# The weights' remainders formed by accumulating DMAs instead of VectorE subtractions, in a two-layer fp32 transformer trunk

## The chip, the cores and the metric

One NeuronCore of a Trainium2 chip. The metric is the device time of one execution in microseconds; for the kernel before it is the median of three runs. The kernel's engines are TensorE (PE: matmuls, and transposes), VectorE (DVE), ScalarE (ACT), GpSimd (POOL) and SyncE (SP), which issues most DMAs.

## The reference

Two layers of a trunk over 512 tokens of 1024 features, in fp32. Each layer has a mixing part and an FFN:

```python
xn = rmsnorm(x, norm1_g[i])
u_pool, q, k, v, g_a, g_b = split(xn @ w_in[i])
# q, k: rmsnorm over 128 features, rotary on the first 32; 4 heads, two softmaxes per head
attn = concat(rmsnorm(softmax1 @ v - lam * softmax2 @ v, subln_g[i])) * (1 - lam_init)   # masked by chunks of 64
pool = (window means of u_pool - u_pool, windows 2, 4, 8, 16) @ pool_w[i] * pool_scale[i]
x = x + (sigmoid(g_a) * pool + sigmoid(g_b) * attn) @ w_out[i]
gate, up = split(rmsnorm(x, norm2_g[i]) @ w_ffn_in[i])                                    # 2 x 2816
x = x + (silu(gate) * up) @ w_ffn_out[i]
```

## The kernel before

**Three matmuls for one product.** The kernel does every fp32 product as three matmuls of a rounded format (fp32r), in which a value keeps 12 significant bits. A value is split into a rounded part, hi, and the remainder lo = value - hi; `product` (L207) adds the stationary operand's hi by the moving one's hi (L215), its hi by the moving one's lo (L216), and its lo by the moving one's hi (L217); the weights are the stationary operand in some products and the moving one in others, as in `w_out`. In a matmul's row the moving operand comes first. So each weight is needed as `whi` and `wlo`.

**The weights.** The host lays all weights out in the order of their use, as 244 pieces of two row tiles by 512 columns, 512 KB each (`weight_plan`). `piece` (L175) loads the next one: a DMA on SP into a tile `raw` (L180, three buffers; the first four pieces lie elsewhere), then `split` (L164): ACT copies `raw` to `whi`, which rounds it (L166), and DVE subtracts, `wlo = raw - whi` (L167). `whi` and `wlo` have eight buffers each, so a piece is split once TensorE is done with the piece eight places earlier. `wblock` gives a block: eight row tiles (four pieces) of `w_in` or `w_ffn_in`; for `w_out` one piece by column half for a single head, and two for the last two heads; the FFN's down projection takes four or three pieces by column half. `split` is also used for activations, so the lines L166 and L167 hold both; the tile's name tells them apart (`whi`/`wlo` are weights).

**The order of the work.** In each layer the heads go in the order 3, 2, 1, 0: `attention` makes q, k, v and the gate of one head, and the steps of its softmax chain are put off by `later` until TensorE has streamed so many columns (`QK_WAIT` and the like), so that TensorE has other matmuls meanwhile. `mix` of the head before makes the pool branch (u; its gate as `ta` by a Tanh on ACT, L485), its product with `pool_w`, then on DVE `ta` by the product (L493) and the sum of both branches (L494), split into `mh` on ACT (L172) and `ml` on DVE (L173), the stationary operands of `w_out` (`project_out`, `add_out`). `project_out` comes for head 3, for head 2 each alone, and for the last two together, after `mix(3)`. Then the FFN in three rounds (`ffn_in`, `swiglu`, `ffn_out`). The program gives this order; a scheduler then sets each engine's own order from it, and an engine takes its instructions strictly in that order.

**The norms** use POOL: DVE makes the mean square (r, L230), POOL raises it to the power -0.5 (L231, "pow"), and DVE scales by it (for q and k: L422, after ACT's squares in L418, then rotary in L286 to L291, and TensorE's transposes, L221). Apart from constants at the start these 80 pows are all that POOL does before the change.

Of the kernel before, what the change touches and what calls it, by code (L numbers as in the profile page):

```python
# [12 lines left out]
AF = mybir.ActivationFunctionType  # L13
ALU = mybir.AluOpType
# [12 lines left out]
ROT = 32  # L27
# [3 lines left out]
EPS = 1e-6  # L31
WINDOWS = (2, 4, 8, 16)
MASKED = -3.0e38
# Hidden tiles of the FFN in three rounds.
ROUNDS = ((0, 8), (8, 16), (16, 22))
# Rows of `rows`, per layer: q gain, k gain, lambda vectors, sub-norm gain.
R_QG, R_LAM, R_SG = 0, 256, 768
ORDER = (3, 2, 1, 0)
# The hidden tiles lie where the attention's tiles lay: from which tile on, under which tag, how many.
HIDDEN_AT = {0: ("qk", 4), 4: ("v", 2), 6: ("u", 2), 8: ("m", 2), 10: ("qk", 4), 14: ("v", 2), 16: ("u", 2), 18: ("m", 2),  # L40
             20: ("qk", 4)}
# How many columns TensorE streams between a step and the one of its chain that follows on TensorE.
QK_WAIT, SCORE_WAIT, PROB_WAIT, AV_WAIT, NORM_WAIT, MERGE_WAIT = 20400, 33600, 25200, 11400, 15000, 15000


def weight_plan():
    """The weight pieces in the order of their use: (name, layer, first row tile, columns)."""
    plan = []

    def block(name, layer, cols, k0=0, k1=KD):  # L50
        for k in range(k0, k1, 2):
            plan.append((name, layer, k, cols))

    def span(*parts):
        return [c for a, n in parts for c in range(a, a + n)]

    def qk(j):
        return span((1024 + 256 * j, 256), (2048 + 256 * j, 256))

    def vg(j):  # L60
        return span((3072 + 256 * j, 256), (5120 + 256 * j, 256))

    def ug(j):
        return span((256 * j, 256), (4096 + 256 * j, 256))

    for layer in range(L):
        def out(heads):
            for cb in range(2):
                for j in heads:
                    block("w_out", layer, span((512 * cb, 512)), 2 * j, 2 * j + 2)  # L70

        for i, j in enumerate(ORDER):
            block("w_in", layer, qk(j))
            if i >= 2:
                out(ORDER[i - 2:i - 1])
            block("w_in", layer, vg(j))
            if i:
                block("w_in", layer, ug(ORDER[i - 1]))
        block("w_in", layer, ug(ORDER[3]))
        out(ORDER[2:])  # L80

        def ffn_in(f):
            block("w_ffn_in", layer, span((P * f, 256), (FF + P * f, 256)))

        def ffn_out(f0, f1):
            for cb in range(2):
                block("w_ffn_out", layer, span((512 * cb, 512)), f0, f1)

        for r, (f0, f1) in enumerate(ROUNDS):
            for f in range(f0, f1, 2):  # L90
                ffn_in(f)
                if r and f == f0:
                    ffn_out(*ROUNDS[r - 1])
        ffn_out(*ROUNDS[-1])
    return plan
# [3 lines left out]
def trunk_kernel(  # L99
# [11 lines left out]
    nc = tc.nc  # L111
# [34 lines left out]
        return row.partition_broadcast(P)  # L146

    def lambdas():
        """The negated weights of the second softmax."""
        for layer in range(L):  # L150
            lam_init = 0.8 - 0.6 * math.exp(-0.3 * layer)
            lv, nl = lams[layer], neglam[layer]
            lp = sb.tile([P, 2, QK], F32, name="lp", tag="qn", bufs=3)
            nc.vector.tensor_mul(lp, lv[:, :, 0, :], lv[:, :, 1, :])
            l2 = const.tile([P, 2], F32, name=f"l2{layer}")
            nc.vector.tensor_reduce(l2, lp, axis=AX.X, op=ALU.add)
            nc.scalar.activation(l2, l2, AF.Exp)
            nc.vector.tensor_sub(nl, l2[:, 1:2], l2[:, 0:1])
            nc.vector.tensor_scalar_add(nl, nl, -lam_init)
# [2 lines left out]
    at = [0]  # L162

    def split(hi, lo, src):  # L164
        """src = hi + lo exactly, each of 12 significant bits."""
        ins = nc.scalar.copy(hi, src)  # L166
        nc.vector.tensor_sub(lo, src, hi.bitcast(F32))  # L167
        return ins

    def split_half(hi, lo, src):  # L170
        """As split, of src / 2."""
        nc.scalar.activation(hi, src, AF.Copy, scale=0.5)  # L172
        nc.vector.scalar_tensor_tensor(lo, src, 0.5, hi.bitcast(F32), op0=ALU.mult, op1=ALU.subtract)  # L173

    def piece(raw=None):  # L175
        i = at[0]
        at[0] += 1
        if raw is None:
            raw = sb.tile([P, 2, 512], F32, name="raw", tag="raw", bufs=3)
        nc.sync.dma_start(raw.rearrange("p a b -> p (a b)"), wts[i])  # L180
        hi = sb.tile([P, 2, 512], F32R, name="whi", tag="whi", bufs=8)
        lo = sb.tile([P, 2, 512], F32R, name="wlo", tag="wlo", bufs=8)
        split(hi, lo, raw)
        return [(hi[:, a, :], lo[:, a, :]) for a in range(2)]

    def wblock(n):
        """n row tiles of 512 columns: (hi, lo) by row tile."""
        return [pair for _ in range(n // 2) for pair in piece()]

    # Work that waits for other engines: (due by TensorE's columns, order, what).  # L190
    clock = [0]
    waiting = []
    count = [0]
# [4 lines left out]
        count[0] += 1  # L198

    def run_due(done=None):  # L200
        """What is due by now, or everything in its order until done()."""
        if running[0]:
            return
        running[0] = True
        while waiting and (waiting[0][0] <= clock[0] if done is None else not done()):
            heapq.heappop(waiting)[2]()
        running[0] = False  # L207
        assert done is None or done()

    def product(acc, pairs):  # L210
        """acc = the sum over pairs of (lhsT hi, lo), (rhs hi, lo)."""
        n = len(pairs)
        for i, ((ah, al), (bh, bl)) in enumerate(pairs):
            run_due()
            nc.tensor.matmul(acc, lhsT=ah, rhs=bh, start=i == 0, stop=False)  # L215
            nc.tensor.matmul(acc, lhsT=ah, rhs=bl, start=False, stop=False)  # L216
            nc.tensor.matmul(acc, lhsT=al, rhs=bh, start=False, stop=i == n - 1)  # L217
            clock[0] += 3 * acc.shape[-1]
# [3 lines left out]
        clock[0] += 2 * P  # L222

    def rsqrt_mean(ss, n, width, times=(1.0,)):
        """times * (ss / n + eps) ** -0.5, the factors each for an equal part of the columns."""
        r = sb.tile([P, width], F32, name="r", tag="r", bufs=4)
        part = width // len(times)
        for i, f in enumerate(times):
            cs = slice(i * part, (i + 1) * part)
            nc.vector.tensor_scalar(r[:, cs], ss[:, cs], 1.0 / (n * f * f), EPS / (f * f), op0=ALU.mult, op1=ALU.add)  # L230
        nc.gpsimd.tensor_tensor(r, r, mhalf[:, :width], op=ALU.pow)  # L231
        return r
# [12 lines left out]
        return [g[:, h * 512:(h + 1) * 512] for h in range(2)]  # L245

    def normed(key, t, xh, xl, g):
        """Token tile t of the residual, over its root mean square and by the gain, transposed into xh + xl."""
        xs = sb.tile([P, D], F32, name="xs", tag="mj", bufs=2)
        ss = small("ss")  # L250
        nc.scalar.activation(xs, res[t], AF.Square, accum_out=ss)  # L251
# [27 lines left out]
        return [sb.tile([P, n, S], F32R, name=name + part, tag=tag, bufs=2) for part in "hl"]  # L279

    def rotate(qn, t):
        """The first ROT of each head's features, in place."""
        ca = cos_t[:, t, :].unsqueeze(1).broadcast_to([P, 4, ROT])
        m1 = sb.tile([P, 4, ROT], F32, name="m1", tag="m1", bufs=2)
        m2 = sb.tile([P, 4, ROT], F32, name="m2", tag="m2", bufs=2)
        nc.vector.tensor_mul(m1, qn[:, :, :ROT], ca)  # L286
        for a in range(2):
            sa = sin_t[:, t, a * HALF:(a + 1) * HALF].unsqueeze(1).broadcast_to([P, 4, HALF])
            b = (1 - a) * HALF
            nc.vector.tensor_mul(m2[:, :, a * HALF:(a + 1) * HALF], qn[:, :, b:b + HALF], sa)  # L290
        nc.vector.tensor_add(qn[:, :, :ROT], m1, m2)  # L291
# [35 lines left out]
    for layer in range(L):  # L327
# [9 lines left out]
            return [(h[:, c0:c1], l[:, c0:c1]) for h, l in pairs]  # L337

        def attention(j, before, then):
            """The head's inputs; its output, (1 + tanh(gate / 2)) * the normed sum, transposed, follows token by token."""  # L340
            if before is not None:
                need(*((layer, before, "s", t) for t in range(NT)))
            qh, ql = pair("q", "qk", 4)
# [105 lines left out]
            return [(hi[:, a, :], lo[:, a, :]) for a in range(2)]  # L449

        def windowed(j, c, acc, uh, ul):
            """The window means less the tile's own values, by shifted sums."""
            window = WINDOWS[j]
            up = sb.tile([P, 16 + S], F32, name="up", tag="up", bufs=2)
            nc.vector.memset(up[:, :16], 0.0)
# [12 lines left out]
            split(uh[:, c, :], ul[:, c, :], prev[:, 16:])  # L468

        def merged(j, mj, mh, ml):  # L470
            """The pool branch and the sum of both branches, transposed."""
            w = wblock(KD)
            pw = pool_weights(j)
            uh, ul = pair("u", "u", 2)
# [121 lines left out]


def constants():
    """What depends on the shapes alone: rotary factors and pool counts, by token."""
    import numpy as np  # L600

    f = np.float32
# [48 lines left out]
```

## Time and profile before

| | |
|---|---|
| median of three runs | 1483.15 us (1483.08 to 1483.3) |
| span of the profiled execution, first to last instruction | 1481.0 us |
| granted TensorE clock | 1.000 |
| DMA: bytes, mean rate | 138.19 MB, 93 GB/s |

The span is what the trace covers; the profiled execution's time stands beside the runs' median as span plus what lies around it, some 2.15 us. A page of the profile gives the busy time of each engine and its share of the span, the same in 40 slices, the DMA queues, the chain of work that ended last, and the costliest groups of instructions (line, engine, operation, out<-in, shape, xcount, then busy us and mean ns of one, then the idle time of the engine ahead of them and what ended it). Rows of the timeline give the start, the duration, the instruction and, in brackets, how long the engine was idle before it and which instruction ended that. Rows of the windows give, for each stretch of time, the busy time (and instructions) of PE, its weight load, DVE, ACT and POOL, then the granted clock, the DMA share and GB/s. Matmuls overlap: one takes 0.39 us, and the next starts 0.23 us after it.

### The profile page before, as it was taken

What the parts mean: (1) busy time and instruction counts of PE and PEld (TensorE: products, weight loads), DVE (VectorE), ACT (ScalarE), POOL (GpSimd) and SP (SyncE); (2) the same over time, 40 slices, a digit from 0 to 9 for tenths busy, and PEclk for the clock granted to TensorE, in tenths of its full rate; (3) what the DMA queues carried; (4) which work ended last, traced back from release to release, by engine and by line L of the source; (5) the groups of instructions that cost most, each with busy time, mean ns of one, the idle gap of its engine ahead of it and who ended that gap; (6) DMA issues with size and microseconds to landing.
All of it is one profiled execution on the core that took longest, in us unless ns stands there. A gap on an engine that the chain in (4) does not pass through costs nothing.

```text
span 1481.0 us, 18060 instructions
## 1 busy us (share of the span) xinstructions
PE 1473.8 (100%) x6998; PEld 1227.6 (83%) x6998; DVE 793.8 (54%) x1550; ACT 531.6 (36%) x1081; POOL 62.3 (4%) x87
## 2 busy tenths in 40 slices
PE   8999999999999999999999999999999999999999
PEld 6888888888988888888888888888889888888887
DVE  7767676566634334433476676766655433434331
ACT  6545343453323222312354543435433322222220
POOL 1010000000000000000010001000000000000000
PEclk9999999999999999999999999999999999999999
DMA  6322231223233223313222232222313223323311
GB/s 245 115 65 79 78 108 59 91 95 98 86 99 114 99 72 114 114 58 113 100 86 71 73 106 65 85 85 86 114 57 115 96 75 114 99 72 114 111 47 57
DMA packets 39832, 138.19 MB, mean 93 GB/s; under 512 B 4545, under 2 KB 5441, under 8 KB 39746
## 3 DMA queue, kind: packets, MB, share of 16 engines
q1 hardware_dynamic: 38450, 134.41, 27.5%
q10 hardware_dynamic: 1296, 2.62, 0.6%
q8 instruction: 55, 0.90, 0.3%
q14 instruction: 31, 0.25, 0.0%
HBM read 134.92 MB, written 2.10 MB: 93 GB/s over the span
## 4 chain that ended last, share of the span: by engine, by line
PE 98%; DVE 1%; ACT 0%; DMA 0%; POOL 0%; issue 0%; POOLq 0%; DVEq 0%; ACTq 0%
PE mm L217 30%; PE mm L215 30%; PE mm L216 30%; PE tr L221 3%; PE sc L217 1%; PE sc L216 1%; PE sc L215 1%; PE oy L217 1%; PE oy L216 1%; PE oy L215 1%; DVE xs L255 0%; DVE wlo L167 0%; ACT xs L251 0%; DMA res<-in_x 0%; DVE res L503 0%; POOL r L231 0%
## 5 line engine op out<-in xcount | busy, mean ns | idle before, releaser
L215 PE MATMUL mm<-xh,whi 128*128 128x512 f32 (+1 forms) x960 | 369.1, 385 | 0.0
L217 PE MATMUL mm<-xh,wlo 128*128 128x512 f32 (+1 forms) x960 | 367.1, 382 | 0.0
L216 PE MATMUL mm<-xl,whi 128*128 128x512 f32 (+1 forms) x960 | 366.9, 382 | 0.0
L166 ACT CAST whi<-raw 128x1024 fp32r<-128x1024 f32 x244 | 255.5, 1050 | 294.0 <-PE mm L217 139.4
L167 DVE TENSOR_TENSOR wlo<-raw,whi 128x1024 fp32r<-128x1024 f32 x244 | 297.5, 1222 | 117.2 <-ACT whi L166 109.0
L217 PEld LDWEIGHTS mm<-xh,wlo 128*128 128x128 f32 x960 | 180.4, 188 | 35.1
L216 PEld LDWEIGHTS mm<-xl,whi 128*128 128x128 f32 x960 | 180.6, 188 | 34.2
L215 PEld LDWEIGHTS mm<-xh,whi 128*128 128x128 f32 x960 | 180.5, 188 | 34.1
L215 PE MATMUL mm<-whi,xh 128*128 128x512 f32 x512 | 205.8, 402 | 0.1
L217 PE MATMUL mm<-whi,xl 128*128 128x512 f32 x512 | 200.9, 392 | 0.0
L216 PE MATMUL mm<-wlo,xh 128*128 128x512 f32 x512 | 200.7, 392 | 0.2 <-DVE wlo L167 0.2
L215 PE MATMUL mm<-whi,fh 128*128 128x512 f32 (+1 forms) x358 | 140.2, 391 | 0.0
L217 PE MATMUL mm<-whi,fl 128*128 128x512 f32 (+1 forms) x358 | 139.7, 390 | 0.0
L216 PE MATMUL mm<-wlo,fh 128*128 128x512 f32 (+1 forms) x358 | 139.1, 389 | 0.0
L503 DVE TENSOR_TENSOR res<-mm,res 128x512 f32<-128x512 f32 (+1 forms) x97 | 66.1, 683 | 132.4 <-PE mm L217 132.1
L217 PEld LDWEIGHTS mm<-whi,xl 128*128 128x128 f32 x512 | 96.3, 188 | 20.9 <-DVE xl L167 0.2
L215 PEld LDWEIGHTS mm<-whi,xh 128*128 128x128 f32 x512 | 96.5, 188 | 18.6 <-ACT xh L166 0.6
L216 PEld LDWEIGHTS mm<-wlo,xh 128*128 128x128 f32 x512 | 96.7, 189 | 18.4 <-DVE wlo L167 0.6
L231 POOL TENSOR_TENSOR r<-r,mhalf 128x1 f32<-128x1 f32 (+1 forms) x80 | 61.6, 770 | 1054.8 <-DVE r L230 979.4
L544 DVE SCALAR_TENSOR_TENSOR th<-th,mm 128x512 f32<-128x512 f32 x42 | 28.9, 688 | 122.9 <-ACT th L543 122.8
L217 PEld LDWEIGHTS mm<-whi,fl 128*128 128x128 f32 x358 | 67.4, 188 | 15.4
L216 PEld LDWEIGHTS mm<-wlo,fh 128*128 128x128 f32 x358 | 67.5, 188 | 15.0
(113 smaller groups left out, 1548.9 us busy)
## 6 DMA issues: line engine op xcount, KB each, us to landing
raw<-in_wts SPq DMA_DIRECT2D x244, 512.0 KB, 4.0
pwr<-in_pool_w ACTq DMA_DIRECT2D x8, 256.0 KB, 2.6
out<-res SPq DMA_DIRECT2D x7, 256.0 KB, 2.0
res<-in_x SPq DMA_DIRECT2D x3, 512.0 KB, 8.3
g<-in_gains SPq DMA_DIRECT2D x3, 512.0 KB, 3.7
res<-in_x ACTq DMA_DIRECT2D x1, 512.0 KB, 3.5
lv<-in_rows SPq DMA_DIRECT2D x2, 256.0 KB, 5.3
qkg<-in_rows SPq DMA_DIRECT2D x2, 128.0 KB, 6.6
```

Of the source, the lines that this page charges most:

```text
L166: ins = nc.scalar.copy(hi, src)
L167: nc.vector.tensor_sub(lo, src, hi.bitcast(F32))
L215: nc.tensor.matmul(acc, lhsT=ah, rhs=bh, start=i == 0, stop=False)
L216: nc.tensor.matmul(acc, lhsT=ah, rhs=bl, start=False, stop=False)
L217: nc.tensor.matmul(acc, lhsT=al, rhs=bh, start=False, stop=i == n - 1)
L221: nc.tensor.transpose(dst, src, ident)
L231: nc.gpsimd.tensor_tensor(r, r, mhalf[:, :width], op=ALU.pow)
L503: nc.vector.tensor_add(res[t][:, cs], here, res[t][:, cs])
L544: nc.vector.scalar_tensor_tensor(th, th, 1.0, gate, op0=ALU.add, op1=ALU.mult)
```

## The change

From the ninth piece on, DVE no longer makes `wlo`. ACT copies `raw` to `whi` as before, and then writes `raw` again, scaled by -1 and rounded the same way, into `wlo`, which so holds -whi. POOL then issues a DMA that reads the same piece out of HBM a second time and adds it onto `wlo` in SBUF: raw - whi. The first eight pieces are split as before. The rest of the diff removes comments and docstrings, so lines of the kernel after stand five lines later from there on (a pow is L236, `ta` L490, `mh` L172 as before).

```diff
         hi = sb.tile([P, 2, 512], F32R, name="whi", tag="whi", bufs=8)
         lo = sb.tile([P, 2, 512], F32R, name="wlo", tag="wlo", bufs=8)
-        split(hi, lo, raw)
+        if i < 8:
+            split(hi, lo, raw)
+        else:
+            nc.scalar.copy(hi, raw)
+            nc.scalar.activation(lo, raw, AF.Copy, scale=-1.0)
+            nc.gpsimd.dma_start(lo.rearrange("p a b -> p (a b)"), wts[i], accum_op=ALU.add)
         return [(hi[:, a, :], lo[:, a, :]) for a in range(2)]
```

## The prediction

> **What bounds the kernel now.** First the head of the profile's page: busy time by engine, the granted clock in 40 slices, the DMA queue of the weights, and the chain of work that ended last by engine.
>
> ```profile
> span 1481.0 us, 18060 instructions
> PE 1473.8 (100%) x6998; PEld 1227.6 (83%) x6998; DVE 793.8 (54%) x1550; ACT 531.6 (36%) x1081; POOL 62.3 (4%) x87
> ...
> PEclk9999999999999999999999999999999999999999
> ...
> q1 hardware_dynamic: 38450, 134.41, 27.5%
> ...
> PE 98%; DVE 1%; ACT 0%; DMA 0%; POOL 0%; issue 0%; POOLq 0%; DVEq 0%; ACTq 0%
> ```
>
> TensorE is the bound at a full clock, and the last chain runs over it for 98%. Then the windows, by stage (attention and FFN of each layer; busy time and instructions by engine):
>
> ```profile
> 16.00:480.00 464.00, 463.86 (x2302) 390.18 (x2302) 293.51 (x660) 195.84 (x459) 30.12 (x38) 1.00 0.29 95
> 480.00:740.00 260.00, 260.00 (x1142) 213.55 (x1141) 102.53 (x119) 68.56 (x81) 1.10 (x2) 1.00 0.28 95
> ```
>
> In neither stage is there a gap to win: 0.14 us of 464, none of 260. Third, who waited for the raw pieces and remainders:
>
> ```profile
>   PEld mm L216: 0.6, 1
>   PE mm L216: 0.2, 1
> ```
>
> TensorE waited for a remainder once, under 1 us, and the first eight pieces, on which the start hangs, are not changed. The DVE work that goes was never on the path. So the question is what the new work makes late.
>
> **What goes and what comes.** The groups of the split, the pows on POOL, and the issue and landing of a raw piece:
>
> ```profile
> L166 ACT CAST whi<-raw 128x1024 fp32r<-128x1024 f32 x244 | 255.5, 1050 | 294.0 <-PE mm L217 139.4
> L167 DVE TENSOR_TENSOR wlo<-raw,whi 128x1024 fp32r<-128x1024 f32 x244 | 297.5, 1222 | 117.2 <-ACT whi L166 109.0
> L231 POOL TENSOR_TENSOR r<-r,mhalf 128x1 f32<-128x1 f32 (+1 forms) x80 | 61.6, 770 | 1054.8 <-DVE r L230 979.4
> ```
> ```profile
> L180 SPq DMA_DIRECT2D raw<-in_wts x244: 327/328/852, 1.1 to 1423.2; - x122
> ...
> DMA to landing us min/median/max: 3.3/4.0/7.6
> ```
>
> DVE loses 236 x 1.222 = 288 us, off the path: gain 0 (at most the 0.6 + 0.2 us above). ACT gains 236 scaled copies. None of that size is in the trace, but on 128x512 a scaled ACTIVATE and a plain CAST take the same:
>
> ```profile
> 138.36 0.62 ACT L166 CAST uh<-us 128x512 fp32r<-128x512 f32 x1 [4.09 <-DVE us L460]
> ...
> 355.64 0.63 ACT L172 ACTIVATE mh<-ta 128x512 fp32r<-128x512 f32 x1
> ...
> 401.95 2.94 ACT L166 CAST whi<-raw 128x1024 fp32r<-128x1024 f32 x3
> ```
>
> So 1.05 us each, or (2.94 - 1.05) / 2 = 0.945 per step in a row: 531.6 + 236 x 1.05 = 779 of 1481 us. ACT is not a bound on the whole; only its order can hurt.
>
> POOL gains 236 issues. Their price isn't in the trace: SP's median is 0.33 us, its dearest 0.85; since another engine issues, I allow 1.0 (298 us with the pows, 20%), and a POOL that can't follow is a rival below. The accumulating transfer isn't there either. A raw piece takes 27.5% x 1481.0 x 127.9 / 134.41 MB / 244 = 1.59 us of the 16 engines; the accumulation reads the remainder too, so between 1.59 and 3.18; I take 3.18, and the share becomes 27.5% + 236 x 3.18 / 1481 = 78%. An FFN stage uses four pieces in 96 matmuls of 260.00 / 1142 us, or 5.46 us a piece; 1.59 + 3.18 = 4.77 fits. Below nothing it can't go: a transfer is only added.
>
> The Trainium skill (Collectives: The Full Stack, "The bandwidth ceiling: the fold count and why AG ≠ RS ≠ AR") says that an add in the DMA engines has two source reads and so half a copy's throughput. It speaks against this change; no row here shows an accumulation, and by it the transfer is the upper of the two bounds.
>
> **The shortest lead.** The first pieces of a w_out block have the least time between splitting and use. ACT, DVE and TensorE there, in layer 0:
>
> ```profile
> 141.97 1.05 ACT L166 CAST whi<-raw 128x1024 fp32r<-128x1024 f32 x1 [0.55 <-PE mm L216]
> ...
> 147.66 1.05 ACT L166 CAST whi<-raw 128x1024 fp32r<-128x1024 f32 x1 [0.51 <-DMA raw<-in_wts]
> ```
> ```profile
> 143.06 3.95 DVE L167 TENSOR_TENSOR wlo<-raw,whi 128x1024 fp32r<-128x1024 f32 x3 [1.49 <-ACT whi L166]
> ```
> ```profile
> 156.16 0.40 PE L216 MATMUL mm<-wlo,mh 128*128 128x512 f32 x1
> 156.40 0.40 PE L217 MATMUL mm<-whi,ml 128*128 128x512 f32 x1
> ```
>
> The two pieces make four copies on ACT: 141.97 + 3 x 0.945 + 1.05 = 145.9 us. TensorE takes the second remainder at 156.16: 10.3 us are left for issue and landing. With 1.0 + 4.0 x 2 = 9.0 it fits; with 1.0 + 7.6 x 2 = 16.2 it is 5.9 us late. Elsewhere the lead is mostly 20 to 30 us (eight buffers ahead). The Trainium skill (DMA: Bandwidth & Descriptors, "Anatomy of one DMA — SWDGE (gpsimd) path") has 2.0 us plus bytes over 436e3 for a GpSimd transfer: an estimate of 3.2 us for 512 KB, which would leave 7 of the 10.3.
>
> POOL's queue holds pows (r, for the norms) and now the DMAs between. Before, from the pows ahead of this w_out block:
>
> ```order
> L231 TENSOR_TENSOR r_1413<-r_1413,mhalf_70 128x1
> L231 TENSOR_TENSOR r_1488<-r_1488,mhalf_70 128x1
> L231 TENSOR_TENSOR r_1616<-r_1616,mhalf_70 128x4
> L231 TENSOR_TENSOR r_1744<-r_1744,mhalf_70 128x4
> L231 TENSOR_TENSOR r_1789<-r_1789,mhalf_70 128x4
> ```
>
> And after, the same pows under new numbers (wlo_1649 and wlo_1656 are the two w_out pieces):
>
> ```order
> L236 TENSOR_TENSOR r_1425<-r_1425,mhalf_70 128x1
> L236 TENSOR_TENSOR r_1500<-r_1500,mhalf_70 128x1
> L188 DMA wlo_1649<-in_wts 128x1024
> L188 DMA wlo_1656<-in_wts 128x1024
> L188 DMA wlo_1902<-in_wts 128x1024
> L188 DMA wlo_1909<-in_wts 128x1024
> L236 TENSOR_TENSOR r_1632<-r_1632,mhalf_70 128x4
> L188 DMA wlo_1916<-in_wts 128x1024
> L188 DMA wlo_1923<-in_wts 128x1024
> L236 TENSOR_TENSOR r_1762<-r_1762,mhalf_70 128x4
> L236 TENSOR_TENSOR r_1807<-r_1807,mhalf_70 128x4
> ```
>
> A pow now waits until the DMAs ahead of it may start. The tightest I find, and its chain:
>
> ```profile
> 186.18 1.08 ACT L166 CAST whi<-raw 128x1024 fp32r<-128x1024 f32 x1
> ```
> ```profile
> 187.40 1.01 POOL L231 TENSOR_TENSOR r<-r,mhalf 128x4 f32<-128x4 f32 x1 [7.67 <-DVE r L230]
> ```
> ```profile
> 189.48 1.21 DVE L167 TENSOR_TENSOR wlo<-raw,whi 128x1024 fp32r<-128x1024 f32 x1
> ...
> 191.69 0.28 DVE L291 TENSOR_TENSOR qn<-m,m 128x128 f32<-128x128 f32 x1
> ```
> ```profile
> 193.11 0.60 PE L221 MATMUL tr<-ident,qn 128*128 128x128 f32 x4
> ```
>
> One more ACT copy, 0.945 us, goes ahead of this pow, but the 1.21 us subtraction between pow and qn goes too, and 193.11 - 191.97 = 1.1 us were spare. Price 0; this spot comes four times.
>
> **Where ACT's order bites.** The end of the last head's mixing: ACT, DVE, TensorE.
>
> ```profile
> 348.45 1.05 ACT L166 CAST whi<-raw 128x1024 fp32r<-128x1024 f32 x1 [0.47 <-PE mm L216]
> 349.81 1.05 ACT L166 CAST whi<-raw 128x1024 fp32r<-128x1024 f32 x1 [0.31 <-PE mm L216]
> 351.17 1.05 ACT L166 CAST whi<-raw 128x1024 fp32r<-128x1024 f32 x1 [0.30 <-PE mm L216]
> 352.83 0.60 ACT L485 ACTIVATE ta<-mm 128x512 f32<-128x512 f32 x1 [0.60 <-PE mm L217]
> 354.53 1.05 ACT L166 CAST whi<-raw 128x1024 fp32r<-128x1024 f32 x1 [1.10 <-DMA raw<-in_wts]
> ```
> ```profile
> 356.17 1.22 DVE L167 TENSOR_TENSOR wlo<-raw,whi 128x1024 fp32r<-128x1024 f32 x1
> 357.31 0.69 DVE L173 SCALAR_TENSOR_TENSOR ml<-ta,mh 128x512 fp32r<-128x512 f32 x1
> ```
> ```profile
> 356.67 0.40 PE L215 MATMUL mm<-whi,mh 128*128 128x512 f32 x1
> ...
> 358.08 0.47 PE L217 MATMUL mm<-whi,ml 128*128 128x512 f32 x1
> 358.38 0.39 PE L216 MATMUL mm<-wlo,mh 128*128 128x512 f32 x1
> ```
>
> TensorE takes the first half of mh at 356.67; it ended at 355.64 + 0.63 = 356.27. Before, ACT there has each cast once, then the two halves of mh:
>
> ```order
> L485 ACTIVATE ta_3377<-mm_3352 128x512
> L166 CAST whi_3630<-raw_3628 128x1024
> L166 CAST whi_3636<-raw_3634 128x1024
> L166 CAST whi_3642<-raw_3640 128x1024
> L485 ACTIVATE ta_3404<-mm_3379 128x512
> L166 CAST whi_3648<-raw_3646 128x1024
> L172 ACTIVATE mh_3244<-ta_3377 128x512
> ```
>
> After, with four scaled copies among them:
>
> ```order
> L490 ACTIVATE ta_3421<-mm_3396 128x512
> L186 CAST whi_3678<-raw_3676 128x1024
> L187 ACTIVATE wlo_3679<-raw_3676 128x1024
> L186 CAST whi_3685<-raw_3683 128x1024
> L187 ACTIVATE wlo_3686<-raw_3683 128x1024
> L186 CAST whi_3692<-raw_3690 128x1024
> L490 ACTIVATE ta_3448<-mm_3423 128x512
> L187 ACTIVATE wlo_3693<-raw_3690 128x1024
> L186 CAST whi_3699<-raw_3697 128x1024
> L187 ACTIVATE wlo_3700<-raw_3697 128x1024
> L172 ACTIVATE mh_3284<-ta_3421 128x512
> ```
>
> The last piece's two copies now both stand ahead of mh, behind a raw piece that lands at 354.5: 354.53 + 0.945 + 1.05 = 356.5, and mh ends at 357.1. so TensorE stalls 0.4 us; ml, no longer behind the 1.22 us subtraction, is not late beyond that. The same order comes in layer 1, where I take 0.3. So 0.7 us, plus twice what that raw piece lands later because accumulations of the pieces ahead run beside it: from 0 to 7.6 - 4.0 = 3.6 us; I take half a plain piece, 0.8, since only part of one overlaps. Sum: 0.7 + 2 x 0.8 = +2.3 us.
>
> TensorE's 94 further semaphore instructions (115 before, 209 after, by the order) I price at nothing: the present ones lie within the 463.86 of 464 us. The dearest step in the rows above, 358.08 to 358.38, is 0.07 us over the usual 0.23, so 94 x 0.07 = 7 us is the outer bound. Other work on ACT comes up to some 2 us later too, with slack as far as I can follow it.
>
> The profiled execution's own time is its span plus some 2.15 us around it (1483.15 - 1481.0), equal to the median. 1483.15 + 2.3 = **1485.4 us**.
>
> **Rivals.** "Same" means within 0.2%, 2.97 us, about what a measurement of this kernel can tell from no change: 1480.2 to 1486.1.
> - *All hidden*: 0 to +1 us, 1483.2 to 1484.2. For: the raw piece lands early enough. Chance 0.27; my forecast (up to +3) 0.25.
> - *ACT's queue costs more* (slower): its casts wait 83 us for raw pieces already (row below), everything in its queue behind; with DMA at 78% the raw piece lands 2 to 3.6 us later, 0.7 + 2 x 2 to 0.7 + 2 x 3.6 = +4.7 to +7.9, 1488 to 1491. It decides from a landing 1.2 us later ((2.97 - 0.7) / 2). Chance 0.24.
> - *The accumulation lands too late* for the four w_out blocks (slower): over 10.3 us after the copies; up to 5.9 x 4 = +24, 1485 to 1507. Chance 0.10.
> - *DMA or POOL as the bound* (slower): more than 5.46 - 1.59 = 3.87 us of DMA per piece, or POOL over 5.46 us per issue. At four times a copy, 6.4: 236 x (1.59 + 6.4 - 5.46) = +600, 2080. Against: two reads make twice. Chance 0.10.
> - *Faster* by over 0.2%: TensorE has no 3 us of waits to give in the rows; only if the lighter DVE frees what they don't show. 0.04, near 1480.
>
> ```profile
> ACT whi L166 <- DMA raw<-in_wts: 83.1, 53, 4.0
> ```
>
> **The numbers.** Faster 0.04; same 0.27 + 0.25 = 0.52; slower 0.24 + 0.10 + 0.10 = 0.44. The range runs from 1482.3 to 1497: below lies little but the gain, above the bound by DMA or POOL and the upper half of the late landing.
>
> **What would show it.** Right: TensorE busy but for some 1 us at two places, waiting for ACT's mh; DVE near 506 us, ACT near 779; a queue of POOL's with 236 transfers; few waits of TensorE for DMA. Wrong: TensorE waiting for DMA at w_out or through the FFN, a DMA share over 90%, POOL busy over half, pows late with qn behind them, or a step between matmuls over 0.23 us throughout.

## The result and the profile after

The changed kernel took 1487.87 us (median of five runs, 1485.21 to 1490.12) against 1483.19 (five runs, 1483.08 to 1483.3): ratio 1.0031, 95% interval 1.0018 to 1.0043. It is slower by some 4.7 us, and its runs spread over 5 us where those of before lie within 0.3. The forecast was 1485.4, in a range of 1482.3 to 1497.

The page of the profiled execution (1488.05 us, span 1486.3): busy times, POOL's and SP's DMA queues (q0, q1), the chain that ended last, the new groups, and the median landing of the DMAs.

```profile
span 1486.3 us, 18576 instructions
PE 1474.9 (99%) x6998; PEld 1228.1 (83%) x6998; DVE 529.2 (36%) x1314; ACT 733.6 (49%) x1317; POOL 268.8 (18%) x323
...
q0 software_dynamic: 33984, 123.75, 43.5%
q1 hardware_dynamic: 38450, 134.41, 26.7%
...
PE 96%; DMA 3%; ACT 0%; DVE 0%; issue 0%; POOL 0%; POOLq 0%
...
L188 POOL DMA_DIRECT2D wlo<-in_wts x236 | 207.0, 877 | 868.2 <-ACT wlo L187 599.3
L187 ACT ACTIVATE wlo<-raw 128x1024 fp32r<-128x1024 f32 x236 | 250.2, 1060 | 150.8 <-PE mm L221 122.1
...
raw<-in_wts SPq DMA_DIRECT2D x244, 512.0 KB, 8.7
wlo<-in_wts POOLq DMA_DIRECT2D x236, 512.0 KB, 9.8
```

Added up one by one, DVE's instructions lost 288 us and ACT's gained 248, as forecast; the page's busy time, in which the overlap of neighbours on an engine counts once, shows 265 and 202. No engine but TensorE is near its limit. But transfers now stand for 3% of the last chain where there were 0%, and a raw piece lands in 8.7 us instead of 4.0. The windows by stage say where (attention and FFN of each layer):

```profile
16.00:480.00 464.00, 462.31 (x2296) 388.62 (x2295) 216.25 (x588) 257.30 (x531) 93.51 (x110) 1.00 0.69 172
480.00:740.00 260.00, 260.00 (x1138) 213.48 (x1137) 45.09 (x68) 108.83 (x126) 41.45 (x48) 1.00 0.79 195
740.00:1220.00 480.00, 477.41 (x2370) 401.69 (x2369) 214.81 (x577) 260.95 (x537) 95.46 (x114) 1.00 0.69 167
```

The FFN, with its DMA share of 0.79, lost nothing: 260.00 of 260. TensorE is idle for 1.69 and 2.59 us in the two attention stages. The timeline of TensorE has its only waits for an accumulation there, and the chain has the four transfers that it waited for (start, duration):

```profile
156.55 0.39 PE L220 MATMUL mm<-whi,mh 128*128 128x512 f32 x1
157.40 0.50 PE L221 MATMUL mm<-wlo,mh 128*128 128x512 f32 x1 [0.45 <-DMA wlo<-in_wts]
157.73 0.39 PE L222 MATMUL mm<-whi,ml 128*128 128x512 f32 x1
...
249.37 0.50 PE L221 MATMUL mm<-wlo,mh 128*128 128x512 f32 x1 [0.99 <-DMA wlo<-in_wts]
...
893.19 0.50 PE L221 MATMUL mm<-wlo,mh 128*128 128x512 f32 x1 [1.10 <-DMA wlo<-in_wts]
...
985.64 0.51 PE L221 MATMUL mm<-wlo,mh 128*128 128x512 f32 x1 [1.49 <-DMA wlo<-in_wts]
```
```profile
146.92 10.43 DMA wlo<-in_wts
...
238.39 10.94 DMA wlo<-in_wts
...
882.05 11.09 DMA wlo<-in_wts
...
974.17 11.43 DMA wlo<-in_wts
```

These are the second remainders of the w_out blocks with the shortest lead (pieces 25, 39, 147, 161). The prediction had 10.3 us there for issue and landing; they took 10.4 to 11.4. The waits sum to 4.03 us, the span grew by 5.3. The starts of the matmuls show the rest: they are 0.23 us apart elsewhere, but 0.85 and 0.33 from 156.55 to 157.40 and on to 157.73, so this place costs 0.72 us where its row has 0.45. Counted so, the four places lose 0.72, 1.25, 1.37 and 1.76 us, 5.1 in all.

What runs beside this pair is in the DMA view of the stretch from 143 to 160 us:

```profile
q0 software_dynamic: 443, 1.63, 51.6%
q1 hardware_dynamic: 521, 1.94, 34.1%
...
raw<-in_wts SPq DMA_DIRECT2D x4, 512.0 KB, 10.7
wlo<-in_wts POOLq DMA_DIRECT2D x4, 512.0 KB, 10.7
```

Within 17 us eight transfers of 512 KB are issued there: the pair, four raw pieces, each issued as ScalarE's copies of the pair and of the next two pieces free a buffer, and two more accumulations. Before, four raw pieces were loaded in the same stretch as well, and landed in 4.2 us:

```profile
raw<-in_wts SPq DMA_DIRECT2D x4, 512.0 KB, 4.2
```

The theory from here on: the pair lands late because it shares the 16 DMA engines with that burst of raw loads. Rivals: an accumulation takes 10 us whatever runs beside it; the accumulations crowd each other all along; ScalarE's longer queue costs the time.

### The profile page after: what moved, and what is told of

Same layout as the page of the kernel before. It is cut to its first block, busy times and chain, and to the rows that moved or that the text cites. A ratio compares the mean times of both kernels' runs of the same rounds, so it can differ in the third digit from the quotient of the medians.

```text
span 1486.3 us, 18576 instructions
## 1 busy us (share of the span) xinstructions
PE 1474.9 (99%) x6998; PEld 1228.1 (83%) x6998; DVE 529.2 (36%) x1314; ACT 733.6 (49%) x1317; POOL 268.8 (18%) x323
## 3 DMA queue, kind: packets, MB, share of 16 engines
q0 software_dynamic: 33984, 123.75, 43.5%
q1 hardware_dynamic: 38450, 134.41, 26.7%
## 4 chain that ended last, share of the span: by engine, by line
PE 96%; DMA 3%; ACT 0%; DVE 0%; issue 0%; POOL 0%; POOLq 0%
PE mm L221 29%; PE mm L220 29%; PE mm L222 29%; DMA wlo<-in_wts 3%; PE tr L226 3%; PE sc L222 1%; PE sc L221 1%; PE sc L220 1%; PE oy L222 1%; PE oy L221 1%; PE oy L220 1%; DMA res<-in_x 0%; ACT xs L256 0%; DVE xs L260 0%; ACT xh L166 0%
## 5 line engine op out<-in xcount | busy, mean ns | idle before, releaser
L188 POOL DMA_DIRECT2D wlo<-in_wts x236 | 207.0, 877 | 868.2 <-ACT wlo L187 599.3
L187 ACT ACTIVATE wlo<-raw 128x1024 fp32r<-128x1024 f32 x236 | 250.2, 1060 | 150.8 <-PE mm L221 122.1
L186 ACT CAST whi<-raw 128x1024 fp32r<-128x1024 f32 x236 | 244.4, 1043 | 48.3 <-DMA raw<-in_wts 33.6
L236 POOL TENSOR_TENSOR r<-r,mhalf 128x1 f32<-128x1 f32 (+1 forms) x80 | 61.9, 774 | 312.7 <-DVE r L235 283.5
L553 DVE SCALAR_TENSOR_TENSOR th<-th,mm 128x512 f32<-128x512 f32 (+1 forms) x44 | 29.0, 663 | 162.0 <-PE mm L222 162.0
```

Of the source, the lines that this page charges most:

```text
L186: nc.scalar.copy(hi, raw)
L187: nc.scalar.activation(lo, raw, AF.Copy, scale=-1.0)
L188: nc.gpsimd.dma_start(lo.rearrange("p a b -> p (a b)"), wts[i], accum_op=ALU.add)
L553: nc.vector.scalar_tensor_tensor(th[:, cs], th[:, cs], 0.5, up[:, cs], op0=ALU.mult, op1=ALU.mult)
```

## The experiments

Times beside each are of the kernel before on the same chips. The edits are to `piece` of the changed kernel, or to one constant.

**Take the eight pieces out.**

```diff
-        if i < 8:
+        if i < 8 or i in (24, 25, 38, 39, 146, 147, 160, 161):
```

> As the changed kernel, but the eight pieces of the four short-lead w_out blocks (24, 25, 38, 39, 146, 147, 160, 161) are split by VectorE as before; the other 228 remainders still come by accumulating DMA. Theory (the loss is TensorE waiting for the second remainder of these blocks, 0.45 + 0.99 + 1.10 + 1.49 = 4.03 us): no wait of TensorE for an accumulation over 0.2 us is left, 1483.2 to 1484.2 us, and the runs lie within 1 us of each other. Rival (ScalarE's longer queue, or the doubled DMA load, costs all along): 1486 us or more, spread as wide as that of the changed kernel.

1482.77 us (11 runs, 1482.61 to 1483.17; before 1483.19; ratio 0.9998, 0.9989 to 1.0006). With 228 of 236 accumulations left, the loss and the spread are gone. TensorE's attention stages are full again, at the same DMA share (0.68 and 0.67):

```profile
16.00:480.00 464.00, 463.82 (x2304) 390.45 (x2303) 221.01 (x592) 254.14 (x527) 90.06 (x106) 1.00 0.68 169
740.00:1220.00 480.00, 480.00 (x2380) 404.41 (x2379) 218.99 (x581) 258.33 (x532) 91.45 (x109) 1.00 0.67 164
```

So it is these eight pieces; a load on the DMA all along or ScalarE's queue would have left a loss.

**Only the eight pieces.**

```diff
-        if i < 8:
+        if i not in (24, 25, 38, 39, 146, 147, 160, 161):
```

> The reverse: only those eight pieces come by accumulating DMA, all others by VectorE as before. If an accumulation takes some 10 us by itself, TensorE waits at the same four places and the time is +3 to +5, 1486 to 1488 us. If the 10 us come from crowding by the other accumulations, the landing is 5 to 8 us, TensorE doesn't wait there, and the time is 1483.0 to 1483.8 us.

1490.36 us (5 runs, 1487.35 to 1492.7; ratio 1.0052, 1.0038 to 1.0065), over the 1486 to 1488 expected. The chain of its profiled execution, the fastest of the five, has three of the four transfers, about as long as in the changed kernel (10.7 to 11.2 us for 10.4 to 11.4); the one at 239 us landed in 9.6 without a wait:

```profile
146.52 11.18 DMA wlo<-in_wts
...
881.38 11.18 DMA wlo<-in_wts
973.59 10.71 DMA wlo<-in_wts
```

The other 228 accumulations are not what makes the pair slow. What is left is its own duration, or the raw loads beside it. Once more, for a second profile:

> The kernel with only the eight short-lead pieces by accumulating DMA, once more, for a second profiled execution (its five times lay between 1487.4 and 1492.7 us). Theory: whatever it is over 1483.2 us is the sum of TensorE's waits at the four blocks, within 1 us; the first profile had 1.10, 1.15 and 0.78 and nothing at the second block. Rival: a part of it lies elsewhere, and the waits don't follow the time.

1488.18 us, 5.2 over the 1482.99 of before beside it; TensorE's waits were 0.94, 0.95 and 1.40, 3.3 us in all (the fourth shows at a weight load only). That is more apart than the 1 us expected. By the starts of the matmuls the four places lose 4.5 us, which is what its span is over that of before (1485.7 for 1481.2); the other 0.7 lies outside the span, around which this kernel spends 2.4 to 2.5 us in every run, where the changed kernel and the one before spend 1.7 to 1.8 (the 2.15 put down ahead of the prediction sets the median of three runs against the span of one execution). Why it does is not shown. That 0.7 is also a part of why this kernel came out above the fully changed one; the rest of that is not explained (their intervals overlap).

**No addition.**

```diff
-            nc.gpsimd.dma_start(lo.rearrange("p a b -> p (a b)"), wts[i], accum_op=ALU.add)
+            nc.gpsimd.dma_start(lo.rearrange("p a b -> p (a b)"), wts[i])
```

> As the changed kernel, but POOL's DMA copies the piece onto the remainder's tile instead of adding it (the addition is left out; same bytes out of HBM, same issue, same order). If reading the old value and adding is what makes the landing long: POOL's queue falls from 2.74 to about 1.6 us of the 16 engines a piece, the landing from 9.8 to 5 to 7 us, no waits of TensorE at the four blocks, 1483.2 to 1484.2 us. If it is the issue from POOL or the doubled HBM traffic: landing 8 to 10 us and 1486 or more.

1482.75 us (11 runs, 1482.49 to 1483.33; ratio 0.9998, 0.9989 to 1.0007). Page and remainder's tile:

```profile
q0 software_dynamic: 33984, 123.75, 24.4%
...
L188 POOL DMA_DIRECT2D wlo<-in_wts x236 | 127.1, 539 | 906.9 <-ACT wlo L187 736.6
...
wlo<-in_wts POOLq DMA_DIRECT2D x236, 512.0 KB, 6.3
```

A copy of the same bytes took 24.4% x 1481.1 / 236 = 1.53 us of the 16 engines, the accumulation 43.5% x 1486.3 / 236 = 2.74: 1.79 times. Its issue cost POOL 0.54 instead of 0.88 us, its landing had a median of 6.3 instead of 9.8. The second read of the weights out of HBM and the issue from POOL are free here; the adding costs. The Trainium skill (Collectives: The Full Stack, "The bandwidth ceiling: the fold count and why AG ≠ RS ≠ AR") puts ReduceScatter, whose add needs two source reads, at half of AllGather, which copies; the 1.79 is near it.

**No DMA at all.** The remainder's tile keeps the negated rounded part:

```diff
-            nc.gpsimd.dma_start(lo.rearrange("p a b -> p (a b)"), wts[i], accum_op=ALU.add)
```

> As the changed kernel without the accumulating DMA: the remainder's tile holds the negated rounded part only (the addition of the weights is left out). ScalarE's order and load are those of the changed kernel. Theory (accumulations landing late are all of it): within 0.5 us of before, 1483.0 to 1483.7. Rival (ScalarE's order, as forecast for the end of the last head's mixing): +0.7 us or more, 1483.9 to 1485, with TensorE waiting for mh near 357 and 1090 us.

1482.93 us (11 runs, 1482.75 to 1483.29; ratio 0.9999, 0.9990 to 1.0008). ScalarE's order, on which the forecast stood, costs nothing that shows. TensorE's waits for mh, from the waits view (us in total, times, longest):

```profile
PEld mm L219 <- ACT mh L172: 0.7, 2, 0.3
```

They are at a weight load, which overlaps the matmuls ahead of it.

**The remainder first.** ScalarE writes it, and the DMA is issued, ahead of the rounded part:

```diff
-            nc.scalar.copy(hi, raw)
             nc.scalar.activation(lo, raw, AF.Copy, scale=-1.0)
             nc.gpsimd.dma_start(lo.rearrange("p a b -> p (a b)"), wts[i], accum_op=ALU.add)
+            nc.scalar.copy(hi, raw)
```

> As the changed kernel, but ScalarE writes the negated remainder before the rounded part, and the DMA is written between the two, so that the second remainder of a short-lead block is ready one ScalarE step (0.95 us) earlier. Theory (late landing): each of the four waits is shorter by 0.95, so 0 + 0.04 + 0.15 + 0.54 = 0.7 is left of 4.0, and the time falls by some 3.3 us, to 1484 to 1485.5. Rival (the load all along): no change, 1487 to 1488.

1484.34 us (11 runs, 1482.86 to 1487.21; ratio 1.0009, 1.0000 to 1.0017), some 1.2 us over before where 0.7 was expected, and 3.5 less than the changed kernel. One ScalarE step more of lead buys back most of the loss. Its profiled execution, the slowest of the eleven, has two waits left, one of them longer than any of the changed kernel:

```profile
156.94 0.50 PE L221 MATMUL mm<-wlo,mh 128*128 128x512 f32 x1 [0.31 <-DMA wlo<-in_wts]
...
983.26 0.51 PE L221 MATMUL mm<-wlo,mh 128*128 128x512 f32 x1 [2.10 <-DMA wlo<-in_wts]
```

By the starts of the matmuls the two places lose 0.6 and 3.9 us, as much as its span grew (1485.4 for 1481.0). Of the 3.9, some 1.6 us come after the wait, in which TensorE runs at half its clock (the last section has the rows).

**One of the pair.**

```diff
-        if i < 8:
+        if i not in (25, 39, 147, 161):
```

> Only the second piece of each of the four short-lead w_out blocks (25, 39, 147, 161) comes by accumulating DMA; the first and all others by VectorE. The raw loads of the pieces after it still run beside. Theory (crowding: the 16 engines serve the raw loads and the two accumulations of the pair by turns, a packet of each): alone it lands in about 1.9 + 8 x (0.33 + 0.16) = 5.8 us, TensorE doesn't wait, 1483.0 to 1483.8 us. Rival (an accumulation takes some 10 us by itself): landing 9 to 10, waits as in the run with both, 1486 us or more.

1483.37 us (11 runs, 1483.1 to 1483.9; ratio 1.0002, 0.9993 to 1.0011): no wait, as the theory has it, but the landing was neither of the two values expected:

```profile
DMA to landing us min/median/max: 8.1/8.3/9.3
```

A single accumulation beside the raw loads takes 8.3 us, not 5.8: serving packets by turns is too kind a picture. Against the second of the pair in the changed kernel it is 1.1 us less at the first place (9.3 for 10.4) and 2.7 to 3.3 less at the others.

**No raw loads beside the pair.**

```diff
-        nc.sync.dma_start(raw.rearrange("p a b -> p (a b)"), wts[i])
+        if i in [f + n for f in (24, 38, 146, 160) for n in range(3, 7)]:
+            nc.vector.memset(raw, 0.01)
+        else:
+            nc.sync.dma_start(raw.rearrange("p a b -> p (a b)"), wts[i])
```

> As the changed kernel, but the four raw pieces that are loaded beside each short-lead pair (27 to 30, 41 to 44, 149 to 152, 163 to 166) are filled by a VectorE memset instead of a DMA (those weights are left out). Theory (crowding by the raw loads and the pair): the second accumulation lands in some 6 to 7 us instead of 10.4 to 11.4, no wait of TensorE there, 1482.7 to 1483.8 us. Rival (the pair alone fills the time, or its own latency): landing 9 us or more, waits at the four places, 1485 or more.

1482.7 us (11 runs, 1482.55 to 1482.88; ratio 0.9997, 0.9988 to 1.0006). The pair at 145 us alone, in this kernel and then in the changed one (the remainder's tile from 144 to 148 us):

```profile
L191 POOL DMA_DIRECT2D wlo<-in_wts x2: 865/878/892, 144.6 to 146.5; - x2
...
DMA to landing us min/median/max: 5.5/6.5/7.6
```
```profile
L188 POOL DMA_DIRECT2D wlo<-in_wts x2: 862/876/889, 145.0 to 146.9; - x2
...
DMA to landing us min/median/max: 7.7/9.1/10.4
```

Without the four raw loads the second lands in 7.6 instead of 10.4 us, and the loss is gone. Sixteen raw loads out of 244, at four places, make the difference: this settles it for the raw loads beside the pair. So the loss needs three things at once, and it went whenever one was taken away: the addition (the copy), the pair (one alone), and the raw loads beside it.

**Less room for POOL's descriptors.** POOL's fourth DMA of a burst sat idle for 4 us though its tile was written. The kernel gives POOL's descriptors 1024 bytes of scratch; half, and then three quarters:

```diff
-    nc = bacc.Bacc("TRN2", target_bir_lowering=False, num_devices=1, dynamic_dma_scratch_size=1024)
+    nc = bacc.Bacc("TRN2", target_bir_lowering=False, num_devices=1, dynamic_dma_scratch_size=512)
```

> As the changed kernel with half the scratch for POOL's DMA descriptors (512 instead of 1024). POOL's fourth DMA of a burst sat idle some 4 us with its tile long written. If that is for want of descriptor space, half of it makes the third or even the second DMA wait as well: over 60 idle stretches of POOL instead of 23, and, if the second of a short-lead block is hit, waits of several us at each of the four blocks, 1490 to 1510. If the space plays no part: as the changed kernel, 1485 to 1490.

> As the changed kernel with 768 instead of 1024 for the scratch of POOL's descriptors. If the scratch holds whole transfers (three at 1024, one at 512, as the idle stretches say), it holds two here: POOL's third DMA of a burst waits, over 60 idle stretches instead of 23 and landings of some 8 us; the pair of a short-lead block is not hit, so 1484 to 1495 us. Rival (POOL already falls behind with two in flight): the FFN's bursts run late, 1500 to 1700.

With 512: 1862.14 us (4 runs, ratio 1.2551, 1.2534 to 1.2568). With 768: 1504.28 us (4 runs, 1.0144, 1.0130 to 1.0158). Both missed their times, 512 by far; 768 came out in the rival's 1500 to 1700, but with its FFN stage full (260.00 of 260) and TensorE's idle time in the attention stages. POOL's idle time that nothing in the profile explains ("issue"), at 1024, 768 and 512, from the waits of each:

```profile
POOL wlo L188 <- issue: 105.4, 23, 6.0
```
```profile
POOL wlo L188 <- issue: 311.6, 71, 7.1
```
```profile
POOL wlo L188 <- issue: 832.7, 136, 9.3
```

With less room fewer are under way: by their issues and landings at most three accumulations at 1024, two at 768 and one at 512. The landing itself gets faster (median 9.8, 8.1, 5.8 us), so one accumulation by itself does not take 10 us; but at 512 the transfers of a burst start only as the one ahead is done. From its timeline of POOL, in the FFN:

```profile
524.93 0.87 POOL L188 DMA_DIRECT2D wlo<-in_wts  x1 [7.93 <-issue]
531.34 0.88 POOL L188 DMA_DIRECT2D wlo<-in_wts  x1 [5.54 <-issue]
537.36 0.87 POOL L188 DMA_DIRECT2D wlo<-in_wts  x1 [5.14 <-ACT whi L186]
```

One in 6.0 to 6.4 us, as in these rows, can't feed an FFN that takes a piece in 5.46. More than 1024 was not tried.

**Each accumulation twice.**

```diff
             nc.gpsimd.dma_start(lo.rearrange("p a b -> p (a b)"), wts[i], accum_op=ALU.add)
+            nc.gpsimd.dma_start(lo.rearrange("p a b -> p (a b)"), wts[i], accum_op=ALU.add)
```

> As the changed kernel, but each accumulation is issued twice (the remainder gets the weights added once too often), the second after the first has landed. The DMA then needs 1.55 + 2 x 2.74 = 7.0 us of its 16 engines a piece, over the 5.46 that TensorE takes for a piece in the FFN: DMA share over 90%, TensorE waiting for DMA all through the FFN, about 236 x (7.0 - 6.0) = +240 us, 1700 to 1800. If accumulations overlap better than their summed engine time says, it stays under 1600.

1851.17 us (4 runs, ratio 1.2486, 1.2467 to 1.2505). The queues' shares:

```profile
q0 software_dynamic: 67968, 247.49, 71.6%
q1 hardware_dynamic: 38450, 134.41, 20.5%
```

92% together, as expected, and a time above the expected 1700 to 1800. The second of each couple waited for the first on POOL (904.5 us in all), so how much of this is bandwidth and how much the serial order is not told apart.

**The changed kernel again.**

> The changed kernel once more, for a second profiled execution (its five times lay between 1485.2 and 1490.1 us). Theory: time less 1483.2 equals the sum of the four waits, within 1 us, at another value than 4.0.

1486.52 us, 3.5 over the 1482.99 beside it. The four waits:

```profile
156.92 0.50 PE L221 MATMUL mm<-wlo,mh 128*128 128x512 f32 x1 [0.20 <-DMA wlo<-in_wts]
...
248.73 0.51 PE L221 MATMUL mm<-wlo,mh 128*128 128x512 f32 x1 [0.84 <-DMA wlo<-in_wts]
...
892.33 0.50 PE L221 MATMUL mm<-wlo,mh 128*128 128x512 f32 x1 [0.85 <-DMA wlo<-in_wts]
...
984.12 0.50 PE L221 MATMUL mm<-wlo,mh 128*128 128x512 f32 x1 [0.81 <-DMA wlo<-in_wts]
```

They sum to 2.70 where the first profile has 4.03, and the times are 1.5 us apart; by the starts of the matmuls 3.8 and 5.1 us are lost, as much as the spans grew. So between these two executions the time follows the landing of four transfers.

## Why the prediction was right or wrong

- **TensorE is the bound, the subtraction's 288 us are worth nothing.** Right: without any DMA, and with a copying one, the kernel is within the measurement of before (0.9999, 0.9998).
- **Prices of the new work.** A scaled copy 1.05 us: measured 1.06. POOL's issue, allowed 1.0: measured 0.88. The accumulation, taken as 3.18 us of the engines: 2.74. DMA share, 78%: 43.5 + 26.7 = 70%. All of the right size, and none of them a bound. The signs given for DVE and ACT, 506 and 779 us, left out that neighbours on an engine overlap: the page has 529 and 734.
- **ACT's order at the end of the last head's mixing, +2.3 us.** Wrong, and this was the forecast's only term. TensorE's idle time there was 0.1 us. The half of mh came when I had said: it ends near 359.4, the whole stretch is 2.3 us later (ScalarE's first copy at 350.76 for 348.45), and 357.1 was forecast. But the order that I showed for ACT was not all that moved; on TensorE two more matmuls (at 358.97 and 359.19) now stand ahead of the first that takes the late mh, and put it off by two steps of 0.23. I used the old time of that matmul, 356.67. And the raw piece there did not land late: ScalarE reached it later than it came. The rival in which ScalarE waits longer for raw pieces had its condition met, a landing 4.7 us later in the median, but not its price: ScalarE's casts waited 33.6 us for raw pieces, where it was 83.1.

```profile
359.19 0.39 PE L221 MATMUL mm<-wlo,mh 128*128 128x512 f32 x1
359.51 0.50 PE L220 MATMUL mm<-whi,mh 128*128 128x512 f32 x1
```

- **The shortest lead, "with 1.0 + 4.0 x 2 = 9.0 it fits".** This is the step that failed. The place, the pieces and the 10.3 us were right; the landing was mis-sized, 10.4 to 11.4 us with the issue, and the issue itself began 0.4 us after the copy's end (146.50 to 146.92), which I had put at nothing. I doubled the median landing of a raw piece, which has mostly its own kind for company. At this place two accumulations meet four raw loads that ScalarE's copies set off; without these loads, the second took 7.6. That case stood among the rivals with a chance of 0.10 and up to 24 us; it came with 5. The prediction named the mechanism, but not as the likeliest.
- **POOL's pows behind DMAs, TensorE's semaphores, DMA as the bound.** Nothing showed of the first two. The third is nearer than its 0.10 made it look: with less room for descriptors the transfers do become the bound.

So the sign and the range were right, the size short by half, and the term that made the size was the wrong one: that 1485.4 lay near the result is luck. The class that I gave most, "same" within 0.2% with 0.52, did not come either: 1487.87 is over its 1486.1, though the interval of the ratio begins just below that line, at 1.0018.

The Trainium skill (DMA: Bandwidth & Descriptors, "Anatomy of one DMA — SWDGE (gpsimd) path") gave an estimate of 3.2 us for such a transfer; the copying ones here took 3.6 at the fastest and 6.3 in the median, the accumulating ones 5.5 and 9.8. As a floor it holds, as a forecast of a landing beside other loads it does not.

## What to carry to other kernels

A transfer's price on an otherwise hidden path is its landing in the company that it meets there: list what the same events set off (here four raw loads) and add it up before comparing with the lead. Compare with the shortest lead in the program, not with the usual one; eight pieces of 236 made the whole loss. And when a scheduler has moved one engine's rows, look at the engine that waits as well before using a time from the old trace.

## What the runs showed of the hardware

An accumulating fp32 DMA of 512 KB from HBM onto SBUF took 1.79 times the engine time of a copy, and 0.88 instead of 0.54 us to issue on POOL. The scratch for POOL's descriptors sets how many are under way: with 1024, 768 and 512 bytes at most three, two and one, and the time was 1488, 1504 and 1862 us.

Where TensorE waits long, its granted clock falls too, and 2.1 us was long enough. In the profile with the remainder first, eight matmuls soon after the wait of 2.10 us took 0.56 to 0.63 us instead of 0.39 and started 0.43 us apart instead of 0.23; the first of them and the one behind the last:

```profile
984.32 0.63 PE L222 MATMUL mm<-whi,ml 128*128 128x512 f32 x1
...
987.70 0.40 PE L221 MATMUL mm<-wlo,mh 128*128 128x512 f32 x1
```

The clock that the trace has for this stretch is 0.50, for 3.4 us. With 768 bytes of scratch there are three such stretches of 3.4 us, each at a wait of 2.2 to 2.4 us; the waits of up to 1.5 us in the changed kernel's attention stages brought none. In the kernel with half the scratch and in that with the doubled accumulation, where TensorE waited up to 20.7 and 12.1 us at a time, the mean clock was 0.924 and 0.925, and TensorE's busy time rose from 1475 to 1571 and 1581 us for the same 6998 matmuls. The Trainium skill (TensorE: Matmul & The Clock Gate, "Part 1: The HAM clock gate (the "warmup" mystery)") puts the return to half rate at an idle window of about 3.4 us; the length of the stretches agrees with that window, but an idle time of 2.1 us already brought one on.
